# The projection and the first MLP product as three 256-column products into one half of an accumulator, with a one-step eviction

## The chip, the core and the metric

The kernel runs on one core of a Trainium2 chip. The metric is the device time of one execution in microseconds (us); smaller is better. The engines of the core run side by side, each through its own instructions in order: TensorE (PE) multiplies, with its weight loads shown apart (PEld); VectorE (DVE), ScalarE (ACT) and GpSimd (POOL) do elementwise work; SyncE (SP) starts most transfers. PE writes into accumulators in PSUM, here tiles of 128 partitions by 512 float32 columns.

## The reference

One block of a sequence model, on 256 tokens with a model width of 2048:

```
n = rms_norm(h, norm_mix_w)
proj = n @ w_in                       # 2048 -> 8208 columns
y_a = gated_deltanet_group(...)       # 8 heads of 128
y_b = hgrn2_group(...)                # 8 heads of 128
h = h + concat(y_a, y_b) @ w_out      # 2048 -> 2048
n = rms_norm(h, norm_ffn_w)
h = h + square(relu(n @ w1)) @ w2     # 2048 -> 8192 -> 2048
out = rms_norm(h, norm_final_w)
```

All inputs and the output are float32. The change touches `n @ w_in` and `n @ w1`.

## The kernel before

**Split products.** PE takes its operands in a reduced float32 format. To keep the precision, each operand is split in two: `hi`, the value rounded to that format, and `lo`, the remainder. A product of the exact operands is then taken as hi·hi + hi·lo + lo·hi. For a weight tile, `split` (L108 to L123) makes `hi` by a cast on ACT (L117) and `lo` by a subtraction on DVE (L118), in pieces of 128x1024. The activations are kept transposed, as `xT` for the projection and `hT` for the MLP: for each block of 128 model columns a tile of 128x512, whose first T = 256 columns are the hi part of the 256 tokens and whose last 256 columns are their lo part.

**The two products that are changed.** Both are computed transposed: the weights are the stationary operand, and the tokens stream. For one block of 128 output features and one block `k` of the 16 blocks of the inner dimension, the kernel issues a pair of matmuls. One has `hi` of the weights as stationary operand and streams all 512 columns of the activations, so that an accumulator's left half collects hi·hi and its right half hi·lo (L281, L704). The other has `lo` of the weights and streams the first 256 columns alone, into the right half (L282, L705). After 16 values of `k`, the sum of the two halves is the result. There are 1024 such pairs in the projection (`project`, 16 heads of 2 calls, each call 2 feature blocks by 16 `k`) and 1024 in the first MLP product (64 feature blocks by 16 `k`). Each matmul has a weight load of its own.

**Eviction.** In the projection ACT copies the right half out of PSUM (L288), DVE adds the left half to it (L289), and a third operation multiplies by the row scales `rB` (L290; on POOL for the gated-delta heads, on DVE for the others). In the MLP ACT copies the right half (L708), DVE adds (L709), and DVE forms relu(v)·v (L710).

**Stages.** First the 16 heads: while PE projects head n + 1, the other engines mix head n, with some matmuls of their own between the projection's (L333 to L364 for the gated-delta heads, L517 to L613 for the others). After the eighth head POOL inverts 64 triangular blocks of 32x32 in 31 steps (`gdn_invert`, L410 to L427; the steps are L419 and L421), the inverse goes through memory and comes back as `Xn`, and `gdn_solve` (from L453 on) uses it on PE, DVE and ACT. Then come the output projection (L659), the first MLP product (L704, L705), the second (L721) and the final norm.

**What sets the order.** The program is written as one stream, and a scheduler with a simulated timeline places the instructions of all engines. A changed instruction can so change the order on every engine, far from the line that was edited. Tiles come from rings of buffers (3 for weight tiles, 3 for pieces of `hi` and `lo`, 4 accumulators `acc`, and from the output projection on 4 more, `accb`).

## Time and profile before

| | |
|---|---|
| time, median of 3 runs (lowest to highest) | 1274.51 us (1274.46 to 1277.93) |
| the profiled execution: its own time, its span | 1277.5 us, 1275.6 us |
| granted TensorE clock, mean over the span | 0.99 of full |
| busy: PE, PEld, DVE, ACT, POOL | 97%, 83%, 67%, 53%, 14% |
| first and last matmul of the projection | 8.3 and 454.3 us |
| first and last `lo` matmul of the first MLP product | 555.8 and 918.3 us |

A row of the views is read so: L is the line of the kernel, then the engine, the operation, the output and the inputs by their names, the shape, the count; behind the first bar the busy time in us and the mean of one in ns; behind the second the idle time of the engine just before, with what ended it. Matmuls are pipelined, and the end of one is modelled: its shown duration is longer than the distance to the next. So the start times are what a rate is read from.

### The profile page before, as it was taken

The page shows a single profiled execution, that of the slowest core. Times are in us where ns is not written, and L with a number is a line of the kernel's source. Part 1 is how long each engine was busy: PE and PEld are TensorE (multiplying, and loading weights), DVE is VectorE, ACT ScalarE, POOL GpSimd, SP SyncE. Part 2 cuts the span into 40 slices and gives each one's busy share as a digit, 9 for nine tenths or more (in the row PEclk, how much of TensorE's full clock was granted, in tenths as well). Part 3 has the DMA queues.
Part 4 walks back from the last instruction along what each step waited for, and adds up shares of the span by engine and source line. Part 5 has one row for each costly group of instructions (what it writes and reads, how often), then busy time and mean ns, then how long its engine had stood idle before and what let it go on. Part 6 is the DMA issues. An engine that isn't in the chain of part 4 may idle for free.

```text
span 1275.6 us, 18490 instructions
## 1 busy us (share of the span) xinstructions
PE 1243.4 (97%) x7290; PEld 1054.2 (83%) x7290; DVE 857.5 (67%) x1200; ACT 674.2 (53%) x972; POOL 178.7 (14%) x224
## 2 busy tenths in 40 slices
PE   6999999998999999999999999999999999999997
PEld 5888888877788887888888888888888888888885
DVE  8789999889978996566555565555555555555556
ACT  7567677655667774555444444444444444444453
POOL 4233433278310130000000000000000000000000
PEclk9999999998999998999999999999999999999999
DMA  7445555543424544455555555555555555555552
GB/s 290 167 154 192 172 177 190 182 141 131 151 101 169 196 165 165 160 203 198 177 187 197 173 191 191 176 195 185 178 198 199 197 195 189 188 191 195 198 203 95
DMA packets 34646, 229.65 MB, mean 180 GB/s; under 512 B 4408, under 2 KB 5184, under 8 KB 7808
## 3 DMA queue, kind: packets, MB, share of 16 engines
q1 hardware_dynamic: 32256, 225.32, 50.1%
q0 software_dynamic: 1728, 2.11, 1.3%
q8 instruction: 57, 0.93, 0.3%
q10 hardware_dynamic: 576, 1.05, 0.2%
q14 instruction: 29, 0.24, 0.1%
HBM read 225.83 MB, written 2.63 MB: 179 GB/s over the span
## 4 chain that ended last, share of the span: by engine, by line
PE 91%; DVE 3%; POOL 3%; issue 2%; DMA 1%; ACT 0%; SPq 0%; POOLq 0%; DVEq 0%; ACTq 0%
PE acc L281 15%; PE acc L721 14%; PE accb L721 13%; PE accb L704 9%; PE acc L704 9%; PE acc L282 8%; PE acc L659 7%; PE accb L705 5%; PE acc L705 5%; POOL Xt L419 1%; POOL X L421 1%; DVE xT L163 1%; DMA big<-in_xt_dram 1%; PE pk L363 1%; DVE E L548 0%
## 5 line engine op out<-in xcount | busy, mean ns | idle before, releaser
L118 DVE TENSOR_TENSOR lo<-w,hi 128x1024 fp32r<-128x1024 f32 x408 | 511.9, 1256 | 362.9 <-ACT hi L117 362.3
L117 ACT CAST hi<-w 128x1024 fp32r<-128x1024 f32 (+1 forms) x416 | 432.7, 1042 | 442.4 <-PE accb L721 177.0
L281 PE MATMUL acc<-xT,hi 128*128 128x512 f32 x1024 | 363.7, 401 | 10.0 <-ACT hi L117 8.3
L282 PE MATMUL acc<-xT,lo 128*128 128x256 f32 x1024 | 283.6, 286 | 4.5 <-DVE lo L118 4.3
L281 PEld LDWEIGHTS acc<-xT,hi 128*128 128x128 f32 x1024 | 192.1, 191 | 50.1 <-ACT hi L117 8.3
L282 PEld LDWEIGHTS acc<-xT,lo 128*128 128x128 f32 x1024 | 195.7, 192 | 11.6 <-DVE lo L118 5.8
L704 PE MATMUL acc<-hT,hi 128*128 128x512 f32 x512 | 181.3, 399 | 0.0
L704 PE MATMUL accb<-hT,hi 128*128 128x512 f32 x512 | 180.8, 398 | 0.0
L721 PE MATMUL accb<-hi,gs 128*128 128x512 f32 x496 | 170.5, 389 | 0.0
L705 PE MATMUL accb<-hT,lo 128*128 128x256 f32 x512 | 143.2, 281 | 0.0
L705 PE MATMUL acc<-hT,lo 128*128 128x256 f32 x512 | 142.8, 281 | 0.0
L721 PE MATMUL acc<-hi,gs 128*128 128x512 f32 x496 | 133.4, 389 | 0.0
L704 PEld LDWEIGHTS accb<-hT,hi 128*128 128x128 f32 x512 | 96.1, 188 | 23.8
L704 PEld LDWEIGHTS acc<-hT,hi 128*128 128x128 f32 x512 | 96.1, 188 | 23.3
L159 POOL TENSOR_TENSOR fin<-fin,cst 128x1 f32<-128x1 f32 x2 | 1.1, 566 | 776.9 <-PE accb L721 769.5
L721 PEld LDWEIGHTS accb<-hi,gs 128*128 128x128 f32 x496 | 93.1, 188 | 19.4
L721 PEld LDWEIGHTS acc<-hi,gs 128*128 128x128 f32 x496 | 93.1, 188 | 19.2
L705 PEld LDWEIGHTS acc<-hT,lo 128*128 128x128 f32 x512 | 96.5, 189 | 0.2
L705 PEld LDWEIGHTS accb<-hT,lo 128*128 128x128 f32 x512 | 96.5, 189 | 0.1
L721 PE MATMUL accb<-lo,gs 128*128 128x512 f32 x248 | 95.8, 389 | 0.0
L721 PE MATMUL acc<-lo,gs 128*128 128x512 f32 x248 | 77.2, 389 | 0.0
L721 PEld LDWEIGHTS accb<-lo,gs 128*128 128x128 f32 x248 | 46.6, 188 | 9.7
(248 smaller groups left out, 1275.2 us busy)
## 6 DMA issues: line engine op xcount, KB each, us to landing
w<-in_w_ff_dram SPq DMA_DIRECT2D x128, 1024.0 KB, 4.9
w<-in_w_in_dram SPq DMA_DIRECT2D x62, 1024.0 KB, 5.0
w<-in_w_out_dram SPq DMA_DIRECT2D x16, 1024.0 KB, 4.9
big<-in_xt_dram SPq DMA_DIRECT2D x4, 512.0 KB, 7.7
w<-in_w_in_dram SPq DMA_DIRECT2D x4, 512.0 KB, 7.9
h<-in_x_dram SPq DMA_DIRECT2D x2, 1024.0 KB, 9.0
dt<-scr_g POOLq DMA_DIRECT2D x8, 128.0 KB, 5.6
nfw<-in_norm_final_w_dram SPq DMA_DIRECT2D x1, 1024.0 KB, 4.4
```

What stands on the lines that cost most here:

```text
L117: ACT.copy(hi, w)
L118: eng.tensor_tensor(out=lo, in0=w, in1=hi.bitcast(F32), op=ALU.subtract)
L163: DVE.scalar_tensor_tensor(out=dst[:, k, T:2 * T], in0=pt, scalar=wcol, in1=dst[:, k, 0:T].bitcast(F32), op0=ALU.mult, op1=ALU.subtract)
L281: PE.matmul(accs[g], lhsT=hi[:, kk, g, :], rhs=xT[:, k, :], start=(k == 0), stop=False)
L282: PE.matmul(accs[g][:, T:], lhsT=lo[:, kk, g, :], rhs=xT[:, k, 0:T], start=False, stop=(k == KT - 1))
L363: PE.matmul(pk0, lhsT=R[:, 1, 0:P], rhs=qk.rearrange("p a t -> p (a t)"), start=True, stop=True)
L419: POOL.tensor_tensor(out=t3, in0=X[:, j, j + 1:].unsqueeze(2).to_broadcast([np_, nr, ncol]), in1=X[:, j, 0:ncol].unsqueeze(1).to_broadcast ...
L421: POOL.tensor_tensor(out=X[:, j + 1:, 0:ncol], in0=X[:, j + 1:, 0:ncol], in1=t3, op=ALU.subtract)
L659: PE.matmul(accs[2 * hf + c], lhsT=st, rhs=ww[:, c * 512:(c + 1) * 512], start=(k == 0 and a == 0 and ww is hi), stop=(k == 2 * NH - 1 and ...
L704: PE.matmul(accs[f], lhsT=hi[:, cs], rhs=hT[:, k, :], start=(k == 0), stop=False)
L705: PE.matmul(accs[f][:, T:], lhsT=lo[:, cs], rhs=hT[:, k, 0:T], start=False, stop=(k == KT - 1))
L721: PE.matmul(accs[hf][c], lhsT=gs[:, a + hf * P:a + hf * P + P], rhs=ww[:, cs], start=(f == 0 and a == 0 and ww is hi), stop=(f == NF - 1 a ...
```

## The change

A helper `product` issues, for one feature block and one `k`, three matmuls of 256 columns, all into the same 256 columns of an accumulator: hi·hi, hi·lo and lo·hi. The right half of the accumulator is no longer used. The `hi` weights are loaded twice, once for each matmul that uses them. The result stands in PSUM in one piece, and the eviction shrinks: in the projection one DVE multiplication by `rB` straight out of PSUM, for all heads; in the MLP a relu on ACT out of PSUM, and one DVE multiplication of that with the accumulator. Nothing else is edited; the scheduler places everything anew.

```diff
@@ -121,6 +121,12 @@
+
+    def product(acc, hi, lo, x2, k):
+
+        PE.matmul(acc, lhsT=hi, rhs=x2[:, 0:T], start=(k == 0), stop=False)
+        PE.matmul(acc, lhsT=hi, rhs=x2[:, T:2 * T], start=False, stop=False)
+        PE.matmul(acc, lhsT=lo, rhs=x2[:, 0:T], start=False, stop=(k == KT - 1))
@@ -263,7 +269,7 @@
     def project(base, hd, chunk, dsts):
-        accs = [acc_a() for _ in range(2)]
+        accs = [acc_a()[:, 0:T] for _ in range(2)]
@@ -278,16 +284,11 @@
                     for g in range(2):
-                        PE.matmul(accs[g], lhsT=hi[:, kk, g, :], rhs=xT[:, k, :], start=(k == 0), stop=False)
-                        PE.matmul(accs[g][:, T:], lhsT=lo[:, kk, g, :], rhs=xT[:, k, 0:T],
-                                  start=False, stop=(k == KT - 1))
+                        product(accs[g], hi[:, kk, g, :], lo[:, kk, g, :], xT[:, k, :], k)
         for g in range(2):
-            lot = mp.tile([P, T], F32, tag="lot", name="lot", bufs=2)
-            ACT.copy(lot, accs[g][:, T:])
-            DVE.tensor_tensor(out=lot, in0=accs[g][:, 0:T], in1=lot, op=ALU.add)
-            (POOL if base == 0 else DVE).tensor_tensor(out=dsts[g], in0=lot, in1=rB, op=ALU.mult)
+            DVE.tensor_tensor(out=dsts[g], in0=accs[g], in1=rB, op=ALU.mult)
@@ -691,7 +692,7 @@
-        accs = [acc_a() if fg % 2 == 0 else acc_b() for _ in range(4)]
+        accs = [(acc_a() if fg % 2 == 0 else acc_b())[:, 0:T] for _ in range(4)]
@@ -701,13 +702,11 @@
-                        PE.matmul(accs[f], lhsT=hi[:, cs], rhs=hT[:, k, :], start=(k == 0), stop=False)
-                        PE.matmul(accs[f][:, T:], lhsT=lo[:, cs], rhs=hT[:, k, 0:T], start=False, stop=(k == KT - 1))
+                        product(accs[f], hi[:, cs], lo[:, cs], hT[:, k, :], k)
         for f in range(4):
-            lot = fp.tile([P, T], F32, tag="lotf", name="lotf", bufs=2)
-            ACT.copy(lot, accs[f][:, T:])
-            DVE.tensor_tensor(out=lot, in0=accs[f][:, 0:T], in1=lot, op=ALU.add)
-            DVE.scalar_tensor_tensor(out=g(4 * fg + f), in0=lot, scalar=0.0, in1=lot, op0=ALU.max, op1=ALU.mult)
+            r = fp.tile([P, T], F32, tag="lotf", name="r", bufs=2)
+            ACT.activation(r, accs[f], AF.Relu)
+            DVE.tensor_tensor(out=g(4 * fg + f), in0=accs[f], in1=r, op=ALU.mult)
```

**Order in the first MLP product, on PE.** Four feature blocks have an accumulator each (`accb` with a number); `hi` and `lo` are pieces of one weight tile. Before, two feature blocks of one `k`, and the first of the next:

```order
L704 MATMUL accb_6219<-hT_4998,hi_6287 128x512
L705 MATMUL accb_6219<-hT_4998,lo_6288 128x256
L704 MATMUL accb_6220<-hT_4998,hi_6287 128x512
L705 MATMUL accb_6220<-hT_4998,lo_6288 128x256
L704 MATMUL accb_6221<-hT_4998,hi_6287 128x512
```

And with the change:

```order
L127 MATMUL accb_7231<-hT_5830,hi_7323 128x256
L128 MATMUL accb_7231<-hT_5830,hi_7323 128x256
L129 MATMUL accb_7231<-hT_5830,lo_7324 128x256
L127 MATMUL accb_7232<-hT_5830,hi_7323 128x256
L128 MATMUL accb_7232<-hT_5830,hi_7323 128x256
L129 MATMUL accb_7232<-hT_5830,lo_7324 128x256
```

The pair of unequal matmuls has become a run of equal ones, three to a feature block.

**Order around the solve, on PE.** `pP` is the first product of the solve and needs `Xn`, the inverse; `pd` and `pa` belong to the mix of the third hgrn head, `pvh` is that mix's first transpose. Before:

```order
L578 MATMUL pd<-E 32x32 x4
L453 MATMUL pP<-Xn,big 32x32
L578 MATMUL pd<-E 32x32 x28
L581 MATMUL pd<-gx 32x64 x8
L587 MATMUL pa<-E 32x32 x4
L591 MATMUL pa<-E 64x64 x2
L593 MATMUL pa<-L 128x128
```

And with the change:

```order
L518 MATMUL pvh<-cst,R 128x128 x2
L579 MATMUL pd<-E 32x32 x2
L454 MATMUL pP<-Xn,big 32x32
L579 MATMUL pd<-E 32x32 x4
L129 MATMUL acc<-xT,lo 128x256 x2
L127 MATMUL acc<-xT,hi 128x256
```

The first matmul that needs the inverse stood behind 780 of the 1024 `lo` matmuls of the projection (24.38 calls of `project`), and now stands behind 760 (23.75 calls); most of the mix's own small matmuls come after it.

**Order ahead of the inversion, on POOL.** `X<-scr_a` loads the blocks that are inverted; `u`, `gx` and `E` belong to the mix of the first hgrn head. Before:

```order
L373 DMA scr_a<-PA_141 32x2x32 x4
L540 TENSOR_TENSOR u<-u 128x256
L543 TENSOR_SCALAR gx<-gx 128x256
L410 DMA X<-scr_a 64x1024
L552 TENSOR_TENSOR E<-gx 128x256
```

And with the change:

```order
L374 DMA scr_a<-PA_141 32x2x32 x4
L411 DMA X<-scr_a 64x1024
L541 TENSOR_TENSOR u<-u 128x256
L544 TENSOR_SCALAR gx<-gx 128x256
L553 TENSOR_TENSOR E<-gx 128x256
```

The load of the blocks no longer stands behind two operations of another head. On SP, the two loads of `h` for the output projection stand ahead of the last five loads of projection weights, where they stood ahead of the last two.

## The prediction

> **What bounds the kernel now.** I read the page first: the engines' busy time, and the chain that ended last.
>
> ```profile
> PE 1243.4 (97%) x7290; PEld 1054.2 (83%) x7290; DVE 857.5 (67%) x1200; ACT 674.2 (53%) x972; POOL 178.7 (14%) x224
> PE 91%; DVE 3%; POOL 3%; issue 2%; DMA 1%; ACT 0%; SPq 0%; POOLq 0%; DVEq 0%; ACTq 0%
> ```
>
> PE carries the chain, with one weight load to each matmul (7290 and 7290). Second, the busy times by stretch, in this order: stretch, PE, PEld, DVE, ACT, POOL, granted clock, DMA share, GB/s. The stretches are the gated-delta heads, the inversion, the heads behind it, and the first MLP product.
>
> ```profile
> 27.00:250.00 223.00, 223.00 (x1252) 190.07 (x1252) 196.47 (x276) 150.82 (x214) 75.73 (x88) 1.00 0.54 176
> 250.00:340.00 90.00, 79.92 (x724) 67.60 (x723) 79.15 (x127) 48.89 (x84) 63.51 (x88) 0.92 0.42 142
> 340.00:454.00 114.00, 114.00 (x1040) 99.74 (x1039) 98.05 (x179) 80.82 (x144) 19.88 (x23) 1.00 0.44 155
> 555.00:918.00 363.00, 363.00 (x2064) 314.97 (x2063) 205.26 (x270) 160.49 (x206) 0.00 (x0) 1.00 0.54 189
> ```
>
> PE is without a gap in three of the four. Only the inversion stretch has idle PE and a lowered clock. So the rate at which PE starts matmuls sets the time, and what ACT, DVE and POOL save counts only between 250 and 340 us. Third, that rate, from start times (us, then the modelled duration). In the MLP product:
>
> ```profile
> 700.06 0.40 PE L704 MATMUL acc<-hT,hi 128*128 128x512 f32 x1
> 700.29 0.28 PE L705 MATMUL acc<-hT,lo 128*128 128x256 f32 x1
> 700.40 0.40 PE L704 MATMUL acc<-hT,hi 128*128 128x512 f32 x1
> ...
> 702.18 0.40 PE L704 MATMUL acc<-hT,hi 128*128 128x512 f32 x1
> ```
>
> Six pairs lie between the first and the last row: 2.12 us, 353.3 ns to a pair. In the projection there are two rhythms:
>
> ```profile
> 60.09 0.40 PE L281 MATMUL acc<-xT,hi 128*128 128x512 f32 x1
> ...
> 61.86 0.40 PE L281 MATMUL acc<-xT,hi 128*128 128x512 f32 x1
> ```
>
> ```profile
> 102.37 0.39 PE L281 MATMUL acc<-xT,hi 128*128 128x512 f32 x1
> ...
> 104.10 0.39 PE L281 MATMUL acc<-xT,hi 128*128 128x512 f32 x1
> ```
>
> Five pairs each: 354 ns and 346 ns. I take 350 ns for the projection, their mean.
>
> **The change part by part.** *The pair of 512 and 256 columns becomes three of 256.* The columns are the same 768; one matmul with its load is added, 2048 times. Everything hangs on the distance between equal 256-column matmuls, which the kernel before never issues for long. The nearest rows are places where the scheduler put four `lo` matmuls in a row:
>
> ```profile
> 588.63 0.64 PE L705 MATMUL accb<-hT,lo 128*128 128x256 f32 x4
> 589.11 0.40 PE L704 MATMUL accb<-hT,hi 128*128 128x512 f32 x1
> ```
>
> ```profile
> 566.44 0.63 PE L705 MATMUL acc<-hT,lo 128*128 128x256 f32 x4
> 566.91 0.40 PE L704 MATMUL acc<-hT,hi 128*128 128x512 f32 x1
> ```
>
> That is 0.48 and 0.47 us for four, 120 and 117.5 ns each. A second way to the price is subtraction, from a steady stream of 512-column matmuls in the second MLP product (12 between these rows):
>
> ```profile
> 942.90 1.07 PE L721 MATMUL acc<-hi,gs 128*128 128x512 f32 x4
> ...
> 945.62 1.07 PE L721 MATMUL acc<-hi,gs 128*128 128x512 f32 x4
> ```
>
> 2.72 us for 12 are 226.7 ns each. The quick rhythm leaves 346 - 226.7 = 119.3 ns for the 256 columns, the slow one 353.3 - 226.7 = 126.6 ns. Half of 226.7 would be 113.3: so a matmul of 256 columns costs more than half of one of 512, and each matmul carries a fixed part. From below, the shortest distance in the rows above bounds it, 0.11 us from 700.29 to 700.40. I take 119.5 ns, between the four-fold runs and by the quick subtraction; a product is then 358.5 ns, against 353.3 and 350.
>
> - First MLP product: 1024 x (358.5 - 353.3) = +5.3 us.
> - Projection: 1024 products, of which I count 880, as some four and a half calls of 32 lie in the inversion stretch, where PE waits anyway: 880 x (358.5 - 350) = +7.5 us.
>
> The fixed part is where a rule may be weighed. The Trainium skill (TensorE: Matmul & The Clock Gate, section "Wait — 56ns, not 53.3ns?") gives matmuls that follow each other N / 2.4 GHz plus about 2.5 ns. By that a third matmul would cost 2.5 ns a product, an estimate of 5 us in all where the rows above make 12.8. This trace doesn't agree: 226.7 ns for 512 columns is some 13 ns over 512 / 2.4.
>
> *The added load.* That a load is covered by the matmul ahead of it is seen in the rows above, since four runs of load and matmul take 0.47 us. What one costs if the cover is gone, 8-column matmuls tell, each with its load of 128 columns:
>
> ```profile
> 57.25 1.81 PE L248 MATMUL pn<-gate,cst 128*128 128x8 f32 x14
> 58.99 0.28 PE L259 MATMUL pgr<-cst,gate 128*8 128x128 f32 x1
> ```
>
> 1.74 us for 14, 124 ns. A load needs about as long as 256 columns stream: after the change PE has no slack left between the two, while a 512-column matmul had 100 ns of it.
>
> *The evictions.* In the MLP, per feature block:
>
> ```profile
> L710 DVE SCALAR_TENSOR_TENSOR g<-lotf 128x256 f32<-128x256 f32 x60 | 22.5, 417 | 0.0
> L709 DVE TENSOR_TENSOR lotf<-acc,lotf 128x256 f32<-128x256 f32 x32 | 12.3, 421 | 0.0
> L708 ACT COPY lotf<-acc 128x256 f32<-128x256 f32 x32 | 11.0, 371 | 6.7 <-PE acc L705 6.7
> ```
>
> ACT's 371 ns copy becomes a relu of the same size, and DVE does one operation of some 421 ns in place of two: 64 x 0.417 = 27 us of DVE are gone. I cost that at nothing, since DVE is busy for 205 of 363 us there and PE never idles; were DVE the bound, it would be up to 27 us. In the projection 64 copies leave ACT; on DVE the multiplication takes the place of the addition; POOL loses its multiplications for the gated-delta heads, DVE its own for the hgrn heads (L290, 32 times):
>
> ```profile
> L290 POOL TENSOR_TENSOR pre<-lot,rB 128x256 f32<-128x256 f32 x24 | 29.1, 1214 | 65.9 <-DVE lot L289 65.9
> L290 DVE TENSOR_TENSOR R<-lot,rB 128x256 f32<-128x256 f32 x28 | 15.0, 535 | 0.2
> ```
>
> PE covers these too, but for the inversion stretch. The new wait is DVE's, on an accumulator's last matmul; behind it on DVE stand the next pieces of `lo`, for which PE waits. In the order two pieces are done ahead of each eviction, 16 products or 5.7 us of PE's work, so I cost it at nothing.
>
> *The inversion stretch.* PE waits there for DVE, and then runs at a lower clock:
>
> ```profile
> PE acc L282 <- DVE lo L118: 4.3, 3, 2.8
> PE pa L593 <- DVE L L567: 2.0, 2, 1.6
> PE pd L578 <- DVE E L563: 1.9, 3, 1.1
> ```
>
> ```profile
> 289.51 0.63 PE L281 MATMUL acc<-xT,hi 128*128 128x512 f32 x1
> 289.93 0.41 PE L282 MATMUL acc<-xT,lo 128*128 128x256 f32 x1
> 290.15 0.63 PE L281 MATMUL acc<-xT,hi 128*128 128x512 f32 x1
> ```
>
> A pair takes 640 ns here. PE's busy time falls 10.1 us short of the 90, and a clock of 0.92 takes 0.08 x 90 = 7 us more: some 17 us of the stretch are lost. An hgrn head frees DVE of 4 x 0.535 = 2.1 us there, and some two and a half heads lie in it: 5 us at most. The chain on POOL also starts earlier:
>
> ```profile
> 247.85 2.14 POOL L373 DMA_DIRECT2D scr_a<-PA  x4 [17.08 <-DVE PA L367]
> 252.90 1.20 POOL L540 TENSOR_TENSOR u<-u 128x256 f32<-128x256 f32 x1 [2.91 <-ACT u L539]
> 255.83 0.59 POOL L410 DMA_DIRECT2D X<-scr_a  x1
> ```
>
> By the order the load of the blocks no longer stands behind `u`: from 255.8 to about 250, 5 us, and POOL takes up L419 only when the load is in. Against that, PE meets the first matmul of the solve 20 products earlier, 20 x 0.35 = 7 us, and everything of PE queues behind it. Where no more than these 7 us is waited for in place of what is lost now, the stretch gains; where the inverse is no earlier, it pays. Bounds: -8 us (the 5 of DVE and 3 of clock) and +4 us (7 less the 3 that PE's waiting already holds). I take -4 us. The two loads of `h`, now ahead of five loads of weights on SP, need the solve's last reader of `PA`, which in PE's order still stands ahead of the products that free SP's own buffers: nothing, or one transfer time of some 9 us if that is late.
>
> *Sum:* +5.3 + 7.5 - 4 = +8.8 us. The profiled execution has 1277.5 us (span 1275.6 and 1.9 around it), so 1286.3; it lies 3.0 us above the median of the runs, which gives **1283 us**.
>
> **The rivals.** *The forecast itself.* With 118.5 to 121.5 ns to a matmul, a product is 355.5 to 364.5: the terms are +7.1 to +24.3, with -4 the time is 1278 to 1295. Chance 0.47; in 0.06 of it the gain of the inversion stretch is at its bound and nothing can be told.
>
> *No difference.* At 117.5 ns, the better of the four-fold runs, a product is 352.5: -0.8 and +2.2, with -4 is 1272 us. For it speaks that run, against it that the other one settles at 120. Chance 0.2, half of it below the bound of what can be told.
>
> *Faster.* If equal matmuls settle at the shortest distance seen, 113 ns, a product is 339: -14.6, -9.7 and -4 make 1246 us. For it speaks that load and stream both fit into it; against it that the distance after a short one was always longer. Chance 0.1.
>
> *Much slower.* If each 256-column matmul carries what the slow rhythm leaves for it, 126.6 ns, a product is 379.8: +27.1 and +26.2 and, as PE then has work for the inversion stretch, 0: 1328 us. This is one mechanism, a clash of load and stream that repeats with each matmul, and it decides from 118 ns on (354 to a product: 1024 x 0.7 + 880 x 4 is +4.2 us, all that the inversion stretch gives back). For it speaks that the MLP product holds the slow rhythm for 360 us; against it the four-fold runs. Chance 0.1.
>
> *The solve pays.* The forecast's rate, but the first matmul of the solve waits for an inverse that is no earlier: +4 in place of -4, 1291 us. Chance 0.12.
>
> *Loads are not covered.* The Trainium skill (TensorE: Matmul & The Clock Gate, section "The mechanism") says that a load overlaps with matmuls in flight only where it is for other rows of the array. Here every load is for all 128 rows. As a mechanism of this kernel: 2048 loads more at 124 ns would be +254 us, 1528 us. By the rows at 588.63 the trace doesn't agree: four loads and four matmuls took 0.48 us. Chance 0.01.
>
> **How the numbers follow.** The likeliest time is 1283. Within 0.3% of 1274.5, about what a measurement here can tell from no change, lie 1270.7 to 1278.3. Faster: 0.1 + 0.1 = 0.2. No difference: 0.1 and 0.06 of the forecast, 0.16. Slower: 0.41 + 0.1 + 0.12 + 0.01 = 0.64. The range of 8 in 10 reaches down to a rate of 117.2 ns with the inversion stretch at its best (-1.7 + 1.4 - 8: 1266) and up to the mild half of "much slower" (122.8 ns, 368.4 to a product: +15.5 + 16.2 and 0 make 1306), and leaves out the rest: 1266 to 1306. The forecast's own range is 1278 to 1295.
>
> **What would show it.** PEld and PE with 9338 each. In the first MLP product, six products from start to start: 2.15 us if a matmul takes 119.5 ns, under 2.12 if the rate gained, 2.28 if the clash repeats; PE's idle time still 0.0, and DVE busy for some 27 us less. In the projection no rhythm of two. In the inversion stretch the wait of `pP` on the inverse, from 0.3 us up to some 5, and less clock lost. I am wrong if three matmuls take less than 353 ns, or if PE idles outside that stretch.

## The result, and the profile after

The changed kernel takes 1287.84 us, the median of 4 runs (1287.70 to 1288.21), beside 1275.22 us for the kernel before (4 runs, 1274.46 to 1277.93). The ratio is 1.0096, with a 95% interval of 1.0078 to 1.0113: it is slower by 1.0%. The profiled execution has 1288.21 us and a span of 1286.3 us, 10.7 us above the span of before. The medians lie 12.6 us apart: the profiled execution of before was 2.3 us above its median, that of the changed kernel 0.4 us.

The page of the changed kernel, busy time of the engines and the chain that ended last:

```profile
PE 1256.0 (98%) x9338; PEld 1163.7 (90%) x9338; DVE 816.3 (63%) x1104; ACT 655.4 (51%) x908; POOL 141.8 (11%) x192
PE 91%; DVE 3%; POOL 3%; issue 2%; DMA 1%; ACT 0%; SPq 0%; POOLq 0%; DVEq 0%; ACTq 0%
```

2048 matmuls and as many loads have come (9338 - 7290). DVE, ACT and POOL are busy for 41, 19 and 37 us less than before, and PE has 91% of the chain as it had. The busy times by stretch, in the same columns as before (PE, PEld, DVE, ACT, POOL, clock, DMA share, GB/s): the gated-delta heads, the inversion, the heads behind it, the output projection, the first MLP product.

```profile
27.00:250.00 223.00, 223.00 (x1776) 215.87 (x1777) 178.57 (x265) 137.38 (x177) 37.69 (x52) 1.00 0.50 172
250.00:340.00 90.00, 78.86 (x896) 75.44 (x894) 79.44 (x118) 47.10 (x74) 66.46 (x92) 0.96 0.43 144
340.00:463.00 123.00, 121.83 (x1330) 118.83 (x1331) 100.44 (x183) 82.21 (x138) 17.11 (x23) 1.00 0.42 151
463.00:559.00 96.00, 96.00 (x611) 78.83 (x609) 61.89 (x84) 51.03 (x75) 6.46 (x8) 1.00 0.49 176
559.00:929.20 370.20, 370.20 (x3089) 370.20 (x3088) 185.62 (x210) 160.25 (x206) 0.00 (x0) 1.00 0.52 185
```

PE is still without a gap in the gated-delta heads and in the MLP product, so what DVE, ACT and POOL saved there bought nothing. The only idle time of PE between 340 and 929 us is 1.2 us right behind 340. The rate of the MLP product, from start times on PE (us, then the modelled duration):

```profile
699.84 0.28 PE L127 MATMUL acc<-hT,hi 128*128 128x256 f32 x1
...
702.00 0.28 PE L127 MATMUL acc<-hT,hi 128*128 128x256 f32 x1
```

18 matmuls, six products, in 2.16 us: 120.0 ns to a matmul, 360 ns to a product, where the pair took 353.3. The same rate holds in the projection, and in the inversion stretch where the clock is full (five products from 289.05 to 290.85 us, 1.80 us). The half rate of the kernel before, 640 ns to a pair, has only moved. It now comes behind a wait of 2.98 us that ends at 295.80:

```profile
296.18 0.42 PE L127 MATMUL acc<-xT,hi 128*128 128x256 f32 x1
...
300.66 0.41 PE L127 MATMUL acc<-xT,hi 128*128 128x256 f32 x1
```

Seven products take 4.48 us, 640 ns each, and the granted clock from 295.8 to 300 us is 0.50.

**Where the time went.** The first and the last start of PE's lines cut each profiled execution into the projection, what lies between it and the first MLP product (the output projection, mainly), and that product. The second product is left out: it takes 347.9 us before and 348.0 after. The rows are ordered by what they have in common; the kernels of the experiments are described below. All times are us, one execution each; the other kernels of the experiments with pairs and three steps have 445.4 to 446.7 us in the projection and 99.8 to 100.8 behind it.

| kernel | products | projection's evictions | projection | between | first MLP product |
|---|---|---|---|---|---|
| before | pairs | three steps | 446.0 | 101.1 | 362.9 |
| MLP only | pairs; MLP three of 256 | three steps | 445.5 | 100.0 | 370.1 |
| groups of 16 in the MLP | pairs | three steps | 445.4 | 100.1 | 357.8 |
| three of 256, long evictions | three of 256 | three steps | 452.7 | 101.4 | 370.1 |
| the change | three of 256 | one step | 454.4 | 95.9 | 370.0 |
| projection only | three of 256; MLP pairs | one step | 455.2 | 95.9 | 362.9 |
| pairs, short evictions | pairs | one step | 447.0 | 95.9 | 356.6 |

Three things are read from it. The MLP product takes 370.0 or 370.1 us wherever it has three matmuls of 256, some 7 us more than the pairs of the kernel before. The projection costs some 7 us more by the products (452.7 against 446.0). And one-step evictions in the projection cost some 2 us inside it with three matmuls (454.4 and 455.2 against 452.7) and up to 1.6 us with pairs (447.0 against 445.4 to 446.7), and bring 4 to 5.5 us behind it: in all kernels that have them the middle takes 95.9 us, in all that don't it takes 99.8 to 101.4. With the start 0.4 us later, the change's own sum against before is +0.4 + 8.4 - 5.2 + 7.1 = 10.7 us, the difference of the spans.

**What happened in the middle.** A part of the chain of waits of the kernel before (start, length, what) shows what the output projection paid there:

```profile
500.69 1.06 ACT hi L117
501.76 1.23 DVE lo L118
502.99 0.35 DVE fsq L397
503.36 0.44 DVE fsq L398
503.82 0.41 ACT yTb L117
504.27 5.49 PE acc L659 x12
```

PE has run out of matmuls. The last head's squares (`fsq`) stand on DVE behind a piece of weights, and PE resumes at 504.27, after 2.9 us of idleness. Then 12 matmuls take 5.49 us, 457 ns each where such a matmul otherwise takes 226.7: PE runs at about half its rate for that long and loses 12 x 0.23 = 2.8 us more. Together 5.7 us, about the 5.2 us by which the middle is shorter in the change. There the same view reads:

```profile
505.38 0.46 PE acc L660 x2
505.85 0.12 PE pm L395
505.96 6.12 PE acc L660 x27
```

PE passes over the last head's end without a gap. The order differs there: `pm`, PE's last matmul for that head, stands behind 159 of the 384 matmuls of the output projection, where it stood behind 180. In the kernels of the table it is 159 with one-step evictions and 180 with three steps. So 21 matmuls more, 4.8 us of PE's work at 226.7 ns, are left to fill the time until the head's result is there. The clock of the stretch is 1.00 in the windows above; of the kernel before, the same view gives 0.97:

```profile
454.30:555.40 101.10, 98.17 (x605) 80.26 (x604) 66.15 (x101) 54.57 (x82) 5.24 (x8) 0.97 0.47 167
```

**The inversion stretch.** The waits of PE in the changed kernel (us in total, times, longest):

```profile
PE acc L129 <- DVE lo L118: 6.9, 4, 3.0
PE poh L613 <- POOL Xt L420: 2.1, 2, 1.8
PE pP L454 <- issue: 2.0, 1, 2.0
```

The waits for the small matmuls `pa`, `pd`, `pvh` and `pm` have shrunk from 5.5 to 1.4 us in sum, and that for `lo` has grown from 4.3 to 6.9 us. New is the wait of the mix's `poh`, whose operand is made on POOL between the inversion's steps. The wait at `pP` isn't one for the inverse, by the timeline:

```profile
338.68 0.53 PE L454 MATMUL pP<-Xn,PA 32*32 32x32 f32 x22
341.17 0.21 PE L454 MATMUL pP<-Xn,PA 32*32 32x32 f32 x1 [1.96 <-issue]
```

The first of the 64 `pP` matmuls ran at 333.47 us without a wait, and the idle time stands before the last of them, where the profile shows nothing that was waited for. PE's idle time from 250 to 340 us is 11.1 us where it was 10.1, with 1.2 us more of this wait behind 340; the clock lost is 0.04 x 90 = 3.6 us where it was 7. So some 17 us of loss have become 16.

### The profile page after: what moved, and what is told of

It is laid out like the page before. It is cut to its first block, busy times and chain, and to the rows that moved or that the text cites. A ratio compares the mean times of both kernels' runs of the same rounds, so it can differ in the third digit from the quotient of the medians.

```text
span 1286.3 us, 22371 instructions
## 1 busy us (share of the span) xinstructions
PE 1256.0 (98%) x9338; PEld 1163.7 (90%) x9338; DVE 816.3 (63%) x1104; ACT 655.4 (51%) x908; POOL 141.8 (11%) x192
## 4 chain that ended last, share of the span: by engine, by line
PE 91%; DVE 3%; POOL 3%; issue 2%; DMA 1%; ACT 0%; SPq 0%; POOLq 0%; DVEq 0%; ACTq 0%
PE acc L720 14%; PE accb L720 13%; PE acc L129 13%; PE acc L128 13%; PE acc L127 13%; PE acc L660 7%; PE accb L129 5%; PE accb L128 5%; PE accb L127 5%; POOL X L422 1%; POOL Xt L420 1%; DVE E L549 1%; DMA big<-in_xt_dram 1%; DVE xT L169 1%; DVE E L564 1%
## 5 line engine op out<-in xcount | busy, mean ns | idle before, releaser
L118 DVE TENSOR_TENSOR lo<-w,hi 128x1024 fp32r<-128x1024 f32 x408 | 501.4, 1230 | 399.7 <-ACT hi L117 398.8
L127 PE MATMUL acc<-xT,hi 128*128 128x256 f32 x1024 | 292.3, 287 | 8.7 <-ACT hi L117 8.7
L129 PE MATMUL acc<-xT,lo 128*128 128x256 f32 x1024 | 290.5, 287 | 7.0 <-DVE lo L118 6.9
L128 PE MATMUL acc<-xT,hi 128*128 128x256 f32 x1024 | 293.2, 287 | 0.0
L127 PEld LDWEIGHTS acc<-xT,hi 128*128 128x128 f32 x1024 | 198.5, 194 | 9.5 <-ACT hi L117 8.7
L128 PEld LDWEIGHTS acc<-xT,hi 128*128 128x128 f32 x1024 | 198.6, 194 | 1.1 <-DVE xT L169 0.2
L127 PE MATMUL acc<-hT,hi 128*128 128x256 f32 x512 | 145.3, 284 | 0.0
L128 PE MATMUL acc<-hT,hi 128*128 128x256 f32 x512 | 144.9, 283 | 0.0
L127 PE MATMUL accb<-hT,hi 128*128 128x256 f32 x512 | 144.9, 283 | 0.0
L128 PE MATMUL accb<-hT,hi 128*128 128x256 f32 x512 | 144.9, 283 | 0.0
L127 PEld LDWEIGHTS accb<-hT,hi 128*128 128x128 f32 x512 | 98.3, 192 | 0.0
L128 PEld LDWEIGHTS accb<-hT,hi 128*128 128x128 f32 x512 | 98.3, 192 | 0.0
```

The costliest lines, as they stand in the source:

```text
L118: eng.tensor_tensor(out=lo, in0=w, in1=hi.bitcast(F32), op=ALU.subtract)
L127: PE.matmul(acc, lhsT=hi, rhs=x2[:, 0:T], start=(k == 0), stop=False)
L128: PE.matmul(acc, lhsT=hi, rhs=x2[:, T:2 * T], start=False, stop=False)
L129: PE.matmul(acc, lhsT=lo, rhs=x2[:, 0:T], start=False, stop=(k == KT - 1))
```

## Experiments

**One half of the change at a time.** First the MLP alone: the projection goes back to the pair and its three steps.

```diff
-                        product(accs[g], hi[:, kk, g, :], lo[:, kk, g, :], xT[:, k, :], k)
+                        PE.matmul(accs[g], lhsT=hi[:, kk, g, :], rhs=xT[:, k, :], ...)
+                        PE.matmul(accs[g][:, T:], lhsT=lo[:, kk, g, :], rhs=xT[:, k, 0:T], ...)
...
-            DVE.tensor_tensor(out=dsts[g], in0=accs[g], in1=rB, op=ALU.mult)
+            (the copy, the addition and the multiplication of before)
```

> Only the first MLP product and its eviction are changed; the projection is that of before. Theory (each 256-column matmul takes its columns' time and a fixed part, 120 ns in all, and PE sets the time): a product goes from 353.3 to 360 ns, 1024 of them make +6.9 us, about 1282 us; the heads, the inversion stretch and the output projection keep their times and their stalls, and the saved DVE and ACT work is worth nothing. Rival (the time of the MLP product is set by its operands' splitting on ACT and DVE, and the loss lies in the projection alone): no change, 1275 us.

Measured: 1283.74 us, ratio 1.0055 (1.0042 to 1.0068). The rows of the two lines that open and close the MLP product, with the first and last start:

```profile
L127 PE MATMUL acc<-hT,hi x512: 278/283/368, 554.1 to 900.9; 128*128 128x256 f32 x171
L129 PE MATMUL accb<-hT,lo x512: 283/283/283, 579.0 to 924.2; 128*128 128x256 f32 x171
```

924.2 - 554.1 = 370.1 us where the pair took 362.9. The loss of 7.0 us by the ratio is the 7.2 us of the stage.

The other half, the projection alone, has the MLP of before:

```diff
-                        product(accs[f], hi[:, cs], lo[:, cs], hT[:, k, :], k)
+                        PE.matmul(accs[f], lhsT=hi[:, cs], rhs=hT[:, k, :], ...)
+                        PE.matmul(accs[f][:, T:], lhsT=lo[:, cs], rhs=hT[:, k, 0:T], ...)
```

> Only the projection and its eviction are changed; the MLP is that of before. Theory: 1024 products of 360 in place of some 350 ns make +10 us, of which the shorter evictions and the new placing give back some 2 us in the inversion stretch and some 5 us at the last heads in the output projection: about +4 us, 1279 us, and with the run that changes the MLP alone it adds up to the whole change (+12.6 us). Rival (the stalls given back depend on the MLP's part too, or the clock does): the two runs don't add up, by over 3 us.

Measured: 1281.62 us, ratio 1.0037 (1.0025 to 1.0050). The projection's last `lo` matmul and the first of the MLP:

```profile
L129 PE MATMUL acc<-xT,lo x1024: 277/283/581, 9.8 to 463.6; 128*128 128x256 f32 x171
L705 PE MATMUL acc<-hT,hi x512: 390/398/482, 559.5 to 899.5; 128*128 128x512 f32 x171
```

The MLP starts 4.1 us later than before, 9.3 us of it lost in the projection and 5.2 given back. The halves add up: 0.55% and 0.37% against 0.96%, so neither part hides the other. The 1281.62 us are 2.6 more than the 1279 expected.

**The products without the short evictions.** The three matmuls stay, and the evictions get the number of operations of before; a maximum of the accumulator with its own copy stands where the two halves were added.

```diff
-            DVE.tensor_tensor(out=dsts[g], in0=accs[g], in1=rB, op=ALU.mult)
...
+            ACT.copy(lot, accs[g])
+            DVE.tensor_tensor(out=lot, in0=accs[g], in1=lot, op=ALU.max)
+            (POOL if base == 0 else DVE).tensor_tensor(out=dsts[g], in0=lot, in1=rB, op=ALU.mult)
...
-            ACT.activation(r, accs[f], AF.Relu)
-            DVE.tensor_tensor(out=g(4 * fg + f), in0=accs[f], in1=r, op=ALU.mult)
...
+            ACT.copy(lot, accs[f])
+            DVE.tensor_tensor(out=lot, in0=accs[f], in1=lot, op=ALU.max)
+            DVE.scalar_tensor_tensor(out=g(4 * fg + f), in0=lot, scalar=0.0, in1=lot, op0=ALU.max, op1=ALU.mult)
```

> The three 256-column products of the change, but evictions with as much work as before: a copy on ACT, an operation of two inputs on DVE (a maximum of a value with its copy, in place of the sum of two halves), then the multiplication on POOL or DVE as before. Theory (the shorter evictions give back the 7 or 8 us of stalls in the inversion stretch and in the output projection): those stalls are back, about 1295 us. Rival (what is given back comes from the new placing alone, and the evictions are covered everywhere): 1288 us, as the changed kernel.

Measured: 1290.76 us, ratio 1.0107 (1.0092 to 1.0123). By the ratios the short evictions are worth 0.0011 x 1276 = 1.4 us, and the intervals overlap, so the time alone doesn't tell it apart from nothing: the 1295 us of the theory didn't come, and the rival is not ruled out by the time. The profiled execution shows two parts that offset each other:

```profile
L129 PE MATMUL acc<-xT,lo x1024: 277/283/582, 10.5 to 461.8; 128*128 128x256 f32 x171
L127 PE MATMUL acc<-hT,hi x512: 278/283/368, 563.2 to 910.0; 128*128 128x256 f32 x171
```

And from the waits of PE (us in total, times, longest):

```profile
PE acc L663 <- ACT yTb L117: 2.9, 1, 2.9
```

The projection is through 1.3 us earlier than in the change, and the 2.9 us of waiting for `yTb` are back, with the order of before around it. This execution was the slowest of its four (1292.80), so the 4.2 us by which its MLP starts later are an upper figure. In the MLP nothing differs: 370.1 us with three operations to a feature block, 370.0 with two. So DVE's and ACT's savings are worth nothing there.

**The short evictions without the products.** The pairs of before, and evictions in one step. Since the right half isn't read, part of the sums is missing from the result; all matmuls run.

```diff
-            ACT.copy(lot, accs[g][:, T:])
-            DVE.tensor_tensor(out=lot, in0=accs[g][:, 0:T], in1=lot, op=ALU.add)
-            (POOL if base == 0 else DVE).tensor_tensor(out=dsts[g], in0=lot, in1=rB, op=ALU.mult)
+            DVE.tensor_tensor(out=dsts[g], in0=accs[g][:, 0:T], in1=rB, op=ALU.mult)
...
+            ACT.activation(r, accs[f][:, 0:T], AF.Relu)
+            DVE.tensor_tensor(out=g(4 * fg + f), in0=accs[f][:, 0:T], in1=r, op=ALU.mult)
```

> The kernel before with its pairs of 512 and 256 columns, but with the one-step evictions of the change, which read the left half of the accumulator alone; the right half is computed and left out of the result, which so lacks the hi by lo and lo by hi terms. It tells what the short evictions are worth where PE's rate is that of before. The first matmul of the solve stands behind 772 lo matmuls of the projection. Theory (the stalls that the changed kernel lost in the inversion stretch and at the last heads go with the shorter evictions): 5 to 8 us less than before, about 1270 us. Rival (PE covers the evictions, and what the changed kernel got back came from how its instructions happened to be placed): within 2 us of before, 1276 us.

Measured: 1266.89 us, ratio 0.9928 (0.9914 to 0.9941), 8.8 us by the medians (the profiled spans differ by 10.6, since that of before lies above its median). The line that opens the MLP, with its first and last start, and the rate inside it:

```profile
L701 PE MATMUL acc<-hT,hi x512: 390/395/482, 551.4 to 885.6; 128*128 128x512 f32 x171
```

```profile
699.81 0.39 PE L701 MATMUL acc<-hT,hi 128*128 128x512 f32 x1
...
702.24 0.40 PE L701 MATMUL acc<-hT,hi 128*128 128x512 f32 x1
```

The MLP starts 4.0 us earlier, by the same middle of 95.9 us; that is the part of the evictions and of the order that comes with them, less than the 5 to 8 us expected. The MLP takes 6.3 us less (356.6, its last start at 908.0), and PE has no idle time there in either kernel: seven pairs take 2.43 us, 347 ns each, where the same pairs took 353.3 in the kernel before. The same instructions run in another rhythm; the next experiments ask why.

This kernel differs from the changed one only by the matmuls and the placing that goes with them. So beside equal evictions the three matmuls cost more than the comparison with before shows: by the ratios 1.0096 and 0.9928 some 21 us, 13.4 of them in the MLP (370.0 against 356.6) and 7.4 in the projection (454.4 against 447.0). Beside the kernel before, the short evictions and its slow rhythm hide a part of that.

**What a matmul costs by its columns.** The MLP with other widths: 192 columns in the feature groups 0 to 4, 384 in 5 to 10, 128 in 11 to 15, three equal matmuls to a product, and one only for the first `k`, so that part of the sums is left out. A single profiled execution, 1319.28 us.

```diff
-                        product(accs[f], hi[:, cs], lo[:, cs], hT[:, k, :], k)
+                        n = (192, 384, 128)[(fg > 4) + (fg > 10)]
...
+                        for ww, st in ((hi, False), (hi, False), (lo, last)):
+                            PE.matmul(full[f][:, 0:n], lhsT=ww[:, cs], rhs=hT[:, k, 0:n], start=False, stop=st)
```

> The changed kernel, but the matmuls of the first MLP product stream 192 columns in the first fifth of the feature groups (0 to 4), 384 in the next (5 to 10) and 128 in the last (11 to 15), three to a feature block and k (one of 256 or 512 columns for the first k); part of the sums is left out, so the output is not that of the block. It tells what the 120 ns of a 256-column matmul are made of. Theory (a fixed part of 13.3 ns beside 0.417 ns to a column, the weight load being covered): 384 columns 173.3 ns; 192 and 128 columns would be 93.3 and 66.7 ns, if the load allows it, and run into the load's own time, 112 to 120 ns, if it doesn't. Rival (the load takes 120 ns and is the bound of 256 columns, the columns themselves have next to no fixed part): 192 and 128 columns 120 ns too, and 384 columns 160 to 165 ns.

The timeline of PE in the three parts, between the same matmul of a product in the first two and over three products in the last (3 matmuls between the first two rows, 12 between the second two, 9 between the last two):

```profile
600.18 0.27 PE L713 MATMUL accb<-hT,lo 128*128 128x192 f32 x1
...
600.52 0.28 PE L713 MATMUL accb<-hT,lo 128*128 128x192 f32 x1
...
699.87 0.33 PE L713 MATMUL acc<-hT,lo 128*128 128x384 f32 x1
...
701.95 0.33 PE L713 MATMUL acc<-hT,lo 128*128 128x384 f32 x1
...
899.94 0.28 PE L713 MATMUL accb<-hT,lo 128*128 128x128 f32 x1
...
900.95 0.27 PE L713 MATMUL accb<-hT,lo 128*128 128x128 f32 x1
```

That is 2.08 / 12 = 173.3 ns for 384 columns, and 0.34 / 3 = 113 and 1.01 / 9 = 112 ns for 192 and 128; over longer runs both come to 111. With 120.0 for 256 and 226.7 for 512, three widths lie on one line: 0.4167 ns to a column and 13.3 ns to a matmul. Below some 234 columns the line would go under 111 ns, and the time stays there. What sets the floor was not varied; the load of 128 columns is what the two widths have in common, so the floor is read as the load's. A matmul of 256 columns is not bound by it. It stands 9 ns above the floor, and a product of three costs more than a pair because it pays the 13.3 ns three times instead of twice: 768 x 0.4167 + 3 x 13.3 = 360, and with two times 13.3 it is 346.7, the quick rhythm.

**Equal matmuls of 512.** The `lo` matmul streams all 512 columns too, and adds them to both halves. A single profiled execution, 1378.94 us, 102.5 more than the 1276.42 of before.

```diff
-                        PE.matmul(accs[f][:, T:], lhsT=lo[:, cs], rhs=hT[:, k, 0:T], start=False, stop=(k == KT - 1))
+                        PE.matmul(accs[f], lhsT=lo[:, cs], rhs=hT[:, k, :], start=False, stop=(k == KT - 1))
```

> The kernel before, but in the first MLP product the lo matmul streams 512 columns too, into both halves (it adds the product of lo with lo, which the block's result hardly feels). All matmuls of the stage are then of one size. Theory (a stream of equal matmuls has 226.7 ns for 512 columns wherever it runs, and the pair of unequal ones loses time by the alternation): 453.3 ns to a pair, the MLP product takes 1024 x 100 = 102 us longer, 1377 us. Rival (the 512-column matmuls of this stage cost 233 to 237 ns by their operands, the alternation has no part in it): 466 to 474 ns, 1390 to 1398 us.

```profile
699.83 0.39 PE L704 MATMUL acc<-hT,hi 128*128 128x512 f32 x1
...
702.09 0.39 PE L704 MATMUL accb<-hT,hi 128*128 128x512 f32 x1
```

Ten matmuls in 2.27 us by the unrounded starts, 226.7 ns each, and 226.7 in every stretch from 570 us to the end of the stage at 1019.7. So equal matmuls show no second rhythm at 512 columns, as they show none at 256, and what the slow rhythm adds belongs to the unequal pair.

**The pair in groups.** If the 6.6 ns of the slow rhythm belong to the alternation, runs of equal matmuls should lose them. In the MLP of before, four of `hi` and then four of `lo`:

```diff
                     for f in range(4):
                         cs = slice(kk * 512 + f * P, kk * 512 + (f + 1) * P)
                         PE.matmul(accs[f], lhsT=hi[:, cs], rhs=hT[:, k, :], start=(k == 0), stop=False)
+                    for f in range(4):
+                        cs = slice(kk * 512 + f * P, kk * 512 + (f + 1) * P)
                         PE.matmul(accs[f][:, T:], lhsT=lo[:, cs], rhs=hT[:, k, 0:T], start=False, stop=(k == KT - 1))
```

> The kernel before, with another order in the first MLP product alone: for each k the four 512-column matmuls with hi, then the four 256-column matmuls with lo. Theory (each matmul takes its own time whatever stands beside it, 226.7 ns for 512 columns and 120 for 256, and the 353.3 ns of the alternating pair hold 6.6 ns that come from the alternation): 346.7 ns to a pair, 1024 of them -6.8 us, about 1268 us. Rival (the pair's 353.3 ns are what 768 columns with two loads cost, whatever the order): 1275 us.

Measured: 1274.95 us, ratio 0.9987 (0.9978 to 0.9995).

```profile
700.04 1.09 PE L704 MATMUL acc<-hT,hi 128*128 128x512 f32 x4
...
705.65 0.63 PE L704 MATMUL acc<-hT,hi 128*128 128x512 f32 x2
```

16 pairs in 5.61 us, 350.6 ns: less than half of the way from 353.3 to 346.7, less than was expected, and the time is nearer to the rival's 1275 than to 1268. If each change of width costs something here, longer runs should cost less. Sixteen of each, a whole weight tile:

```diff
+            parts = [split(w[:, q * 1024:(q + 1) * 1024], 1024) for q in range(2)]
+            for part in range(2):
...
+                            if part == 0: (the matmul with parts[q][0])
+                            else:         (the matmul with parts[q][1])
```

> The kernel before, with the first MLP product in groups of sixteen: all 512-column matmuls with hi of one weight tile, then all its 256-column matmuls with lo. In groups of four a pair took 350.9 ns. Theory (time is lost where matmuls of unequal size meet, and runs of equal ones settle at 226.7 and 120 ns): 347 to 348.5 ns to a pair, 5 to 6.5 us less than before, 1270 us. Rival (the size of the groups is without effect, what was won with four is all): 350.9 ns, 1273.5 us.

Measured: 1271.23 us, ratio 0.9960 (0.9946 to 0.9973).

```profile
700.50 3.82 PE L706 MATMUL acc<-hT,hi 128*128 128x512 f32 x16
704.16 2.08 PE L708 MATMUL acc<-hT,lo 128*128 128x256 f32 x16
706.07 0.63 PE L706 MATMUL acc<-hT,hi 128*128 128x512 f32 x2
```

Sixteen of 512 columns take 3.66 us (228.8 ns each) and sixteen of 256 take 1.91 us (119.4): 348.1 ns to a pair, and the stage takes 357.8 us in place of 362.9. This kernel is faster than both the kernel before and the changed one. It isn't the fastest: the plain alternation in its quick rhythm, which changes the width at every matmul, took 356.6 us for the stage in the kernel with pairs and short evictions. So a change of width doesn't cost something everywhere, and what the runs bring here is read as getting out of the slow rhythm.

The same in the projection, in groups of eight, on top of it:

```diff
                     for g in range(2):
                         PE.matmul(accs[g], lhsT=hi[:, kk, g, :], rhs=xT[:, k, :], start=(k == 0), stop=False)
+                for kk in range(4):
+                    k = kh * 8 + q * 4 + kk
+                    for g in range(2):
                         PE.matmul(accs[g][:, T:], lhsT=lo[:, kk, g, :], rhs=xT[:, k, 0:T], ...)
```

> As the run with groups of sixteen in the MLP, and the projection in groups of eight (the eight 512-column matmuls with hi of one piece, then its eight with lo). Theory: the projection's pairs go from some 350 to 348.5 ns, 1 to 2 us less again, 1268 to 1269 us, if the stalls at the inversion stay as they are. Rival (a lo piece that is late now holds up eight matmuls less early, or the new placing costs more than it gives): 1270 us or more.

Measured: 1273.41 us, ratio 0.9980 (0.9971 to 0.9989), no better than the groups in the MLP alone. Eight pairs of the projection take 2.79 us, from 101.55 to 104.34, or 349.1 ns a pair. Ungrouped pairs take 348.2 ns on average (724 pairs of before that follow each other without another matmul between), so nothing was to be won there; the projection takes 446.4 us against 445.4.

**What switches the rhythm.** In the kernel before, the MLP product runs at 346.7 ns from 568 to 588 us, where the scheduler put four of 512 and four of 256 in a row, and at 353.3 from there to its end. The kernel that changes the projection alone has the same run at 592 us and turns slow there too. In the kernel with pairs and short evictions that place is missing and the quick rhythm stays. An earlier run of four and four, at 565 us, stands ahead of the quick rhythm in the kernel before. So the order of the MLP before was disturbed at three places: feature group 4 in twos, group 8 in fours, group 12 in twos, for one `k` each. A single profiled execution, 1274.10 us.

```diff
+                    group = {4: 2, 8: 4, 12: 2}.get(fg, 1) if k == 4 else 1
+                    for f0 in range(0, 4, group): (group matmuls of hi, then group of lo)
```

> The kernel before, with the order of the first MLP product disturbed at three places, each for one k of one group of feature blocks: in group 4 two matmuls with hi and then two with lo, twice; in group 8 four with hi and then four with lo; in group 12 as in group 4. The scheduler of the kernel before has itself put one run of four and four into group 1, and behind it a pair takes 353.3 ns to the end of the stage, ahead of it 346.7. Theory (an alternating pair has two rhythms that hold themselves, and what happened last decides between them): the rate changes at one or more of the disturbed places and at no other, with nothing but 346.7 and 353.3 ns between them; by the projection's rows two and two are followed by the quick rhythm, four and four by the slow one, so 353.3 up to group 4, 346.7 to group 8, 353.3 to group 12, 346.7 behind it. Rival (the rate hangs on the buffers' places or on what ACT and DVE do meanwhile): 353.3 ns in the whole stage but for the disturbed places themselves.

The timeline of PE after the first disturbance, across the second, after it and after the third:

```profile
699.77 0.40 PE L708 MATMUL acc<-hT,hi 128*128 128x512 f32 x1
...
701.89 0.40 PE L708 MATMUL acc<-hT,hi 128*128 128x512 f32 x1
...
741.46 1.09 PE L708 MATMUL acc<-hT,hi 128*128 128x512 f32 x4
742.39 0.63 PE L710 MATMUL acc<-hT,lo 128*128 128x256 f32 x4
...
779.61 0.39 PE L708 MATMUL accb<-hT,hi 128*128 128x512 f32 x1
...
782.04 0.39 PE L708 MATMUL acc<-hT,hi 128*128 128x512 f32 x1
...
859.90 0.40 PE L708 MATMUL accb<-hT,hi 128*128 128x512 f32 x1
...
862.02 0.40 PE L708 MATMUL accb<-hT,hi 128*128 128x512 f32 x1
```

Six pairs in 2.12 us (353 ns) at 700, seven in 2.43 us (347) at 780, six in 2.12 us again at 860. The rate is slow from the scheduler's own run at 588 us, stays so through the twos at 651, becomes quick at the fours at 741 and slow again at the twos at 830. The states hold themselves for some 90 to 150 us, and change only at a disturbance, so the rival falls. Which disturbance leads to which state had been expected otherwise; twos did nothing once and switched once, and what decides it stays open. The starts also show where the slow rhythm loses its time. From 750 to 825 us the next matmul starts 230.0 ns after one of 512 columns and 116.7 ns after one of 256; from 660 to 735 us it is 236.7 and 116.7. All of the difference lies behind the matmul of 512.

## Why the prediction was right, and where it was not

The direction and its cause were right: PE's matmul rate sets the time, and the rate got worse. The time came out 5 us above the forecast of 1283, within the 1278 to 1295 given for it. In differences, 8.8 us were forecast and 12.6 measured, since the kernel before had 1274.51 us when the forecast was made and 1275.22 beside the changed one. By its steps:

- *The price of a matmul of 256 columns*, taken at 119.5 ns: 120.0 measured. The step that read the quick subtraction (119.3) was sound, the one at 117.5 was a rounding of 0.47 us. The subtraction from the slow rhythm, 126.6, was wrong for equal matmuls: what it carried belongs to unequal pairs, as the runs with equal widths show, and in them it lies behind the matmul of 512 columns: in both rhythms the next one starts 116.7 ns after one of 256. Only the size was a little off.
- *First MLP product*, +5.3 us: mis-sized, +7.2 in the two profiles, shown again alone at +7.0. Half a nanosecond to a matmul is 1.5 us over 3072 of them. Some 0.4 us more come from the pairs of before, which did not all take 353.3 ns: from 568 to 588 us, some 56 pairs, they were in the quick rhythm.
- *Projection*, +7.5 us, from 880 of 1024 products: some +7 by the kernel with long evictions (452.7 against 446.0, and 445.4 to 446.7 in the other kernels with pairs and three steps). The pair, taken at 350 ns from two rows, has 348.2 on average, and the product, taken at 358.5, has 359.2 to 359.7: some 11 ns more, which for 1024 products would be 11.6 us. Some 5 of them are not seen in the length of the projection. The inversion stretch accounts for about 2 (with long evictions PE idles there for 9.9 us at a clock of 0.94, before for 10.1 at 0.92), and where the rest goes is not shown. So leaving out what lies in that stretch was right in direction, but that the size came out is luck: a dearer difference and a larger share left out offset each other.
- *Inversion stretch*, -4 us: this step failed in its place, and that its size fits is luck. The short evictions shortened nothing there. With pairs the projection is 1 us longer with them, with three matmuls 2 us (447.0 against 446.0; 454.4 and 455.2 against 452.7). The gain of 4 to 5.5 us came in the output projection, in a wait of 2.9 us and a half-rate run behind it. The prediction read four stretches and left out the one from 454 to 555 us, so its sentence that savings count only between 250 and 340 us was wrong, and the trace of before showed it. The cause by which it was argued, the earlier load of the blocks, did not come true either. On POOL the load now goes out at 255.32 us, against 255.83:

```profile
251.78 2.14 POOL L374 DMA_DIRECT2D scr_a<-PA  x4 [15.63 <-DVE PA L368]
255.32 0.54 POOL L411 DMA_DIRECT2D X<-scr_a  x1 [1.40 <-DMA scr_a<-PA]
```

  The operation `u` is out of its way, as the order says, but the store of `PA` itself comes at 251.78 instead of 247.85, 3.9 us later, which fits PE's slower products ahead of it. An order tells what a step stands behind, not when that is done.
- *Evictions in the MLP*, costed at nothing: right. Two operations or three to a feature block, the stage takes 370.0 or 370.1 us. The one DVE operation is as long as forecast:

```profile
L709 DVE TENSOR_TENSOR g<-acc,r 128x256 f32<-128x256 f32 x32 | 12.3, 420 | 0.3
```

  DVE's busy time in the stretch is 20 us less, not 27. Busy time counts the overlap of neighbouring records once: in the row of L710 before, 60 operations of 417 ns, 25.0 us, stand for 22.5. The sum of the single durations falls by 26 us.
- *The added load*, covered by the matmul ahead of it: right. It was taken at 124 ns from matmuls of 8 columns, with no slack left; the sweep puts the floor at 111 ns, so 9 ns of slack remain. Why those of 8 columns took longer is not shown.
- *What would show it*: 9338 on both sides, no gap of PE in the MLP, no rhythm of two in the projection, less clock lost in the inversion stretch: all seen. Six products take 2.16 us, 2.15 was said. The wait of `pP`, said to grow from 0.3 to at most 5 us, is 2.0 us, but the profile shows no wait for the inverse in it: its 2.0 us stand before the last of 64 matmuls, the 0.3 of before stood amid them. It reaches 1.2 us beyond 340 us, so by the letter PE idles outside the stretch, which was named as a sign of being wrong; it changes nothing in the account of the rate.

The rivals: *no difference* and *faster* fall with 120.0 ns, *much slower* with the equal matmuls at 256 and 512 columns, *loads are not covered* with the sweep. *The solve pays* falls too: the first matmul of the solve ran without a wait for the inverse. What is left of it is that the projection as a whole got 1 to 2 us longer with the short evictions.

Not settled is whether the middle is shorter because the last head's eviction ends earlier or only because the scheduler then fills PE's queue otherwise, with 159 matmuls ahead of the head's end in place of 180. All kernels with one-step evictions have the shorter middle and all with three steps don't, but both things change together.

## What to carry to other kernels

Where PE has no gap, cost a change of its matmuls by their number as well as their columns: here 13.3 ns for each and 0.4167 ns for each column, and not under 111 ns; splitting one of 512 into two of 256 costs 13.3 ns, whatever it saves on the other engines. A saving on those engines is worth what PE waits for them: look through the whole span for waits of PE that end in the edited chain, since the gain here lay 50 us behind the stage that was edited. Look also at the rhythm of what you compare with: against the slow pair the three matmuls cost 6.7 ns a product, against the quick one 13.3. And where matmuls of two widths alternate in the slow rhythm, try them in runs: sixteen and sixteen in the MLP brought 0.4% here, at the price of no instruction, while runs of eight in the projection brought nothing more.

## What was not expected of the hardware

An alternation of 512 and 256 columns has two rhythms, 346.7 and 353.3 ns to a pair, that hold themselves for tens of microseconds; a run of equal matmuls can switch from one to the other. The quick one is the sum of the two matmuls by the line; the slow one adds 6.6 ns to each pair, behind the matmul of 512 columns. A program whose order changes elsewhere can gain or lose close to 2% of such a stage by this alone: the kernel with pairs and short evictions gained 6.3 of 362.9 us.

The line itself has a fixed part of 13.3 ns. The Trainium skill (TensorE: Matmul & The Clock Gate, section "Wait — 56ns, not 53.3ns?") has matmuls start N / 2.4 ns apart plus about 2.5 ns. The slope agrees, 0.4167 ns to a column; the fixed part does not, 13.3 ns for these operands with a load to each matmul.

The floor of 111 ns for 128 and 192 columns is about one load. The Trainium skill (TensorE: Matmul & The Clock Gate, section "LDWEIGHTS (loading the stationary operand)") gives a load as its columns / 1.2, 106.7 ns for 128; the sweep agrees within 5 ns, and shows that the loads run beside the matmuls although all of them use all rows of the array.
